# One Hymba layer on one core: the output projection as two groups of 1024 columns, with block sums made in DRAM

## The chip, the cores and the metric

The kernel runs on one core of one Trainium2 chip. The metric is the device time of one execution in microseconds (us); the kernel before has a median of 661.75 us in three runs (661.68 to 662.39). Everything is float32 in DRAM.

## The reference, cut to what matters

One layer for 512 tokens and a model width of 2048: an RMS norm, one input projection to 4608 columns, eight attention heads (two key and value heads) beside a gated linear recurrence (LRU) of width 1024, each group normed and gated, and one output projection with the residual.

```python
h = rms_norm(x, norm_w)                                  # 512 x 2048
q, k, v, g_attn, xr, g_lru = split(h @ w_in)             # w_in 2048 x 4608
attn_out = attention_group(q, k, v, q_norm_w, k_norm_w)  # 512 x 1024
lru_out = lru_group(xr, conv_w, conv_b, ...)             # 512 x 1024
mixed = concat([rms_norm(attn_out, attn_norm_w) * silu(g_attn),
                rms_norm(lru_out, lru_norm_w) * silu(g_lru)])
return x + mixed @ w_out                                 # w_out 2048 x 2048
```

## The kernel before, in words

Every product is made in three matmuls of split operands: a float32 operand is cast to a rounded form `hi` (on ACT) and the rest `lo` = operand - `hi` is taken (on DVE), and `hi hi`, `hi lo` and `lo hi` are added in PSUM. For weights this is `wsplit` (L209 the cast `wh`, L210 the difference `wl`), with buffers that TensorE releases.

The program has these stages: the input projection with the transposes and the norm of x; the LRU half by half beside the projections of its gate input, keys and values, and queries; attention beside the projections of the gates (names `fill`, `gates`); then the group norm of attention; the last gate projection; and the output projection from 495.03 us on. TensorE has work all the time, since projections are woven into the rest. The order on each engine is made by the scheduler of the language at build time from the order of the program and from priorities (`tc.high_priority(AHEAD)` and `SOON` move work ahead); each engine then works its list strictly in order. SP issues the loads, POOL does a few small operations (L261 and L262: scale, add and power of -0.5, which is an inverse root).

The group norm (`group_rstd`, `rows`): eight matmuls with ones (L662) bring the sums of squares `asum` into PSUM; DVE copies them to `r_a` (L666); POOL makes the inverse root (L261, L262); DVE makes `part` (L272, L273) and from these two diagonal tiles `s` (L275); TensorE turns the tiles into rows (L281) and DVE copies them to `gbc` (L282), by which the attention tiles are scaled (`normed`, L673). Between `group_rstd` and `rows` TensorE has three steps of six matmuls of the projection `fill`.

The output projection multiplies the mixed values (K = 2048 as eight row pairs of 2 x 128) with `w_out` by Winograd's form of Strassen's scheme: a pair's 2 x 2 blocks are combined into seven products P1, Q6, Q5, Q7, P2, Q3, Q4 in place of eight. The blocks of the mixed side are combined by `build` (function `seven`: sums in a tile `t`, L691 to L698; casts `mh`, L706; differences `ml`, L707). The four LRU pairs `hp` are built first, between steps of the projection that follows `rows`; the attention pairs `ap_` follow after their gate. The blocks of `w_out` are combined on DVE. The first 1024 columns are made as two groups of 512 by `outputs` (six pairs by Winograd with halves of 256 columns: 252 matmuls 128x256 for each group, and two pairs plainly: 48 matmuls 128x512). The other 1024 columns are one group of two halves of 512 by `outputs_wide`: 336 matmuls 128x512 in two passes over the pairs (P1, Q6, Q5, then Q3, P2, Q7, Q4). A gate is a sigmoid on ACT and two products on DVE (`gate`, L648, L652, L653); `evac` (L380) takes a projection out of PSUM.

Within attention, POOL scales each tile of weights (L588) before TensorE transposes it (L595).

## Time and profile before

| what | us |
|---|---|
| median of three runs | 661.75 |
| lowest, highest | 661.68, 662.39 |
| the profiled execution | 660.99 |
| its span | 659.2 |
| TensorE busy | 652.4 |
| DVE, ACT, POOL busy | 500.8, 337.4, 58.9 |
| output stage | 495.03 to 654.01 |

The profiled execution's own time is 1.8 us longer than its span, the stretch from its first to its last recorded event. Busy times are sums over an engine's instructions. A row of the time order has start, duration, engine, line, operation, what is written and read, and in brackets the idle time before it with the instruction that ended it. Grouped rows end with busy time, mean ns and the idle time before.

### The profile page before, as it was taken

To read this page: it belongs to the slowest core of one execution; us is meant where nothing else is said; L and a number is where in the kernel's file an instruction comes from. 1 tells how busy PE (TensorE), PEld (TensorE's weight loads), DVE (VectorE), ACT (ScalarE), POOL (GpSimd) and SP (SyncE) were. 2 spreads that over 40 slices of the span, in tenths; PEclk is the share of its full clock that TensorE was granted. 3 is DMA by queue.
4 is the path that set the end of the run, shared out by engine and by line. 5 is a ranking of instruction groups with operands and counts; after the bars stand their busy time and mean duration, and the time that the engine had idled before them with its cause. 6 is when DMAs were issued, how large, how long until landed. Compare 5 with 4: busy or idle time off the path is not lost.

```text
span 659.2 us, 8994 instructions
## 1 busy us (share of the span) xinstructions
PE 652.4 (99%) x3323; PEld 553.2 (84%) x3323; DVE 500.8 (76%) x822; ACT 337.4 (51%) x582; POOL 58.9 (9%) x79
## 2 busy tenths in 40 slices
PE   8999999999999999999999999999999999999996
PEld 6888888888888888888888888888889999888875
DVE  5889788978688854656955677439989998777995
ACT  3534898589766416444743455335437433233431
POOL 0000000000023303011222212110000000000000
PEclk9999999999999999999999999999999999999999
DMA  8852252323234312322112211232336356375643
GB/s 290 287 142 84 69 164 66 94 64 96 72 121 129 108 53 64 96 65 64 38 60 64 65 45 53 64 96 76 103 110 211 127 178 224 110 230 201 243 140 127
DMA packets 43963, 77.32 MB, mean 117 GB/s; under 512 B 2968, under 2 KB 13328, under 8 KB 43920
## 3 DMA queue, kind: packets, MB, share of 16 engines
q1 hardware_dynamic: 43600, 76.22, 37.5%
q10 hardware_dynamic: 320, 0.53, 0.3%
q8 instruction: 26, 0.43, 0.3%
q14 instruction: 17, 0.14, 0.1%
HBM read 72.54 MB, written 4.19 MB: 116 GB/s over the span
## 4 chain that ended last, share of the span: by engine, by line
PE 98%; DMA 1%; DVE 0%; ACTq 0%; DVEq 0%; issue 0%
PE pj L148 20%; PE pj L150 20%; PE pj L149 20%; PE pj L851 7%; PE pj L752 5%; PE mm L851 5%; PE mm L752 4%; PE mm L148 3%; PE mm L150 3%; PE mm L149 3%; PE mm L765 3%; PE mm L595 2%; PE mm L235 1%; PE pj L301 1%; PE mm L538 1%; DMA wr<-in_w_in_dram 1%
## 5 line engine op out<-in xcount | busy, mean ns | idle before, releaser
L148 PE MATMUL pj<-x,wh 128*128 128x512 f32 x376 | 149.1, 396 | 0.0
L150 PE MATMUL pj<-x,wl 128*128 128x512 f32 x376 | 147.0, 391 | 0.0
L149 PE MATMUL pj<-x,wh 128*128 128x512 f32 x376 | 146.5, 390 | 0.0
L210 DVE TENSOR_TENSOR wl<-wr,wh 128x512 fp32r<-128x512 f32 x144 | 100.8, 722 | 30.0 <-ACT wh L209 29.9
L209 ACT CAST wh<-wr 128x512 fp32r<-128x512 f32 x143 | 85.8, 618 | 73.4 <-PE pj L150 25.7
L150 PEld LDWEIGHTS pj<-x,wl 128*128 128x128 f32 x376 | 70.6, 188 | 15.3
L149 PEld LDWEIGHTS pj<-x,wh 128*128 128x128 f32 x376 | 70.7, 188 | 13.6 <-DVE x L238 0.2
L148 PEld LDWEIGHTS pj<-x,wh 128*128 128x128 f32 x376 | 70.6, 188 | 13.3
L148 PE MATMUL pj<-wh,x 128*128 128x512 f32 x192 | 74.9, 390 | 0.0
L150 PE MATMUL pj<-wh,x 128*128 128x512 f32 x192 | 74.7, 389 | 0.0
L149 PE MATMUL pj<-wl,x 128*128 128x512 f32 x192 | 74.7, 389 | 0.0
L841 ACT CAST wh<-wr 128x1024 fp32r<-128x1024 f32 (+1 forms) x24 | 28.7, 1198 | 52.0 <-PE mm L851 28.6
L597 ACT CAST b<-mm 128x512 fp32r<-128x512 f32 x32 | 18.8, 586 | 61.5 <-PE mm L595 61.5
L583 DVE TENSOR_REDUCE mx<-mm 128x1 f32<-128x512 f32 x32 | 22.0, 689 | 32.9 <-PE mm L150 32.3
L150 PEld LDWEIGHTS pj<-wh,x 128*128 128x128 f32 x192 | 36.0, 188 | 7.6
L148 PEld LDWEIGHTS pj<-wh,x 128*128 128x128 f32 x192 | 36.0, 188 | 7.5
L149 PEld LDWEIGHTS pj<-wl,x 128*128 128x128 f32 x192 | 36.0, 188 | 7.4
L588 POOL TENSOR_SCALAR k<-k,sm 128x512 f32<-128x512 f32 x32 | 24.2, 756 | 123.9 <-DVE sm L587 112.4
L842 DVE TENSOR_TENSOR wl<-wr,wh 128x1024 fp32r<-128x1024 f32 (+1 forms) x24 | 33.5, 1395 | 1.5 <-ACT wh L841 1.3
L598 DVE TENSOR_TENSOR b<-mm,b 128x512 fp32r<-128x512 f32 x32 | 22.1, 689 | 12.1 <-ACT b L597 12.1
L752 PE MATMUL pj<-wh,ml 128*128 128x256 f32 x96 | 27.2, 283 | 0.0
L752 PE MATMUL pj<-wl,mh 128*128 128x256 f32 x96 | 27.2, 283 | 0.0
(249 smaller groups left out, 1350.7 us busy)
## 6 DMA issues: line engine op xcount, KB each, us to landing
wr<-in_w_in_dram SPq DMA_DIRECT2D x71, 512.0 KB, 3.7
wr<-in_w_out_dram SPq DMA_DIRECT2D x40, 512.0 KB, 3.9
b<-in_x_dram SPq DMA_DIRECT2D x7, 512.0 KB, 8.9
out_dram<-xt SPq DMA_DIRECT2D x12, 256.0 KB, 3.2
xt<-in_x_dram SPq DMA_DIRECT2D x8, 256.0 KB, 5.0
wr<-in_w_out_dram SPq DMA_DIRECT2D x8, 256.0 KB, 4.3
t<-in_x_dram SPq DMA_DIRECT2D x4, 512.0 KB, 4.4
k<-in_lru_wa_dram SPq DMA_DIRECT2D x8, 128.0 KB, 3.6
```

Of the source, the lines that this page charges most:

```text
L148: nc.tensor.matmul(acc, lh, rh, start=start, stop=False)
L149: nc.tensor.matmul(acc, lh, rl, start=False, stop=False)
L150: nc.tensor.matmul(acc, ll, rh, start=False, stop=stop)
L209: copy(hi, raw[:, k, :])
L210: nc.vector.tensor_sub(lo, raw[:, k, :], f(hi))
L583: nc.vector.tensor_reduce(mx, sc, axis=AX.X, op=ALU.max, negate=True)
L588: nc.gpsimd.tensor_scalar(p, p, sm, 0.0, op0=ALU.mult, op1=ALU.add)
L598: nc.vector.tensor_sub(ptl[:, :, tt], p3, f(pth[:, :, tt]))
L752: nc.tensor.matmul(dst, lh[:, a, ts_], rh[:, b_, :], start=bank in fresh, stop=last and s == 1 and rh is bh and lh is al, skip_group_check ...
L841: nc.scalar.copy(hi, blocks)
L842: nc.vector.tensor_sub(lo, blocks, f(hi))
L851: nc.tensor.matmul(dst[s], lh[:, ts_], rh, start=i == 0 and j == 0, stop=i == 7 and j == 2)
```

## The change

All 2048 output columns go through one form: `outputs(0)` and `outputs(1)`, each 1024 columns in halves of 512, with all eight pairs by Winograd's form. The first pass holds P1, Q6, Q5, Q7 in all eight banks of PSUM (24 matmuls a pair), the second Q3, P2, Q4 (18 a pair): 2 x 8 x 42 = 672 matmuls of 512 columns, where there were 504 of 256 and 432 of 512.

Some sums of `w_out` blocks are made in DRAM. T3 (`t30`, `t31`, for both groups) and T1 (`t1`, group 0 alone) begin as copies from DRAM to DRAM on SP (24 of 256 KB), woven into the projections of the LRU stage. A transfer on POOL's queue that adds to its destination makes T3 (16, at the same place) and T1 (8, after the last queries' inverse roots and ahead of attention). T2, a sum that DVE makes in the first pass, is stored to DRAM on POOL's queue and read back in the second. The residual x and the outputs of group 0 go over POOL's queue too.

A gate takes Silu in place of the sigmoid, and one operation on DVE in place of two. The builds of the four LRU pairs stand ahead of `group_rstd` in the program, and the pools of attention are closed, and the pool `fin` opened, before it. Pairs 6 and 7 are built by `seven` as the others; `last_sums` is gone.

```diff
+    loads_done, powers = {}, []
     def wraw(w, r0, c0, nk=1, queue=nc.sync):
...
-            queue.dma_start(raw[:, ks, :], src[:, ks, :])
+            loads_done[queue] = queue.dma_start(raw[:, ks, :], src[:, ks, :]).ins
...
         nc.gpsimd.tensor_scalar(dst, src, 1.0 / n, EPS, op0=ALU.mult, op1=ALU.add)
-        nc.gpsimd.tensor_tensor(dst, dst, nhalf[:, :width], op=ALU.pow)
+        powers[:] = [nc.gpsimd.tensor_tensor(dst, dst, nhalf[:, :width], op=ALU.pow).ins]
...
-                    nc.scalar.activation(s, src, AF.Sigmoid)
+                    nc.scalar.activation(s, src, AF.Silu)
             s = ss[e] if sig is k2 else ss[0]
             yield 4
             dst = pairs[e // 2][:, e % 2, :]
-            nc.vector.scalar_tensor_tensor(g, g, v1(row + e), s, op0=ALU.mult, op1=ALU.mult)
-            nc.vector.tensor_mul(dst, dst, g)
+            nc.vector.scalar_tensor_tensor(dst, dst, v1(row + e), s, op0=ALU.mult, op1=ALU.mult)
...
+    split_of = [0]
+    def split(blocks):
+        i = split_of[0] % 4
+        split_of[0] += 1
+        hi, lo = (
+            pools["out" if i else "fin"].tile([P, 2, SEQ], F32R, tag=f"{t}{i}", bufs=1, name=nm(t))
             for t in ("wh", "wl")
...
+        hi, lo = (t[:, : blocks.shape[1]] for t in (hi, lo))
+        nc.scalar.copy(hi, blocks)
+        nc.vector.tensor_sub(lo, blocks, f(hi))
+        return hi, lo
...
+    dram = ctx.enter_context(tc.tile_pool(name="dram", bufs=1, space=bass.MemoryType.DRAM))
+    t1, t2, t30, t31 = (
+        dram.tile([NP, P, SEQ + 16], F32, name=t, tag=t)[:, :, :SEQ] for t in ("t1", "t2", "t30", "t31")
+    )
+    t3 = (t30, t31)
+    def block(m, k, c, n=1):
+        return w_out[(2 * m + k) * P : (2 * m + k + 1) * P, c * SEQ : (c + n) * SEQ]
+    def sums_of_blocks():
+        for m in range(NP):
+            with tc.issue_after(loads_done[nc.sync]):
+                for g in range(2):
+                    nc.sync.dma_start(t3[g][m], block(m, 0, 2 * g))
+                nc.sync.dma_start(t1[m], block(m, 0, 0))
+            for g in range(2):
+                nc.gpsimd.dma_start(t3[g][m], block(m, 1, 2 * g), accum_op=ALU.add)
+            yield
+    def other_sums():
+        with tc.issue_after(*powers):
+            for m in range(NP):
+                nc.gpsimd.dma_start(t1[m], block(m, 0, 1), accum_op=ALU.add)
+    def outputs(g, places, work):
...
+        p1, q6, q5, q7 = banks(*((mm, mm, pj, pj), (pj, mm, mm, pj))[g])
         for i in range(8):
+            m = mixed[i][0] // (2 * P)
+            with tc.high_priority(SOON):
+                x_, y_ = next(places)(), next(places)()
+                if g == 0:
+                    nc.sync.dma_start(x_[:, 0], t1[m])
+                    nc.sync.dma_start(x_[:, 1], block(m, 0, 1))
+                else:
+                    nc.sync.dma_start(x_.rearrange("p j e -> p (j e)"), block(m, 0, 2 * g, 2))
+                    nc.vector.tensor_add(x_[:, 0], x_[:, 0], x_[:, 1])
+                nc.sync.dma_start(y_[:, 0], block(m, 1, 2 * g))
+                nc.sync.dma_start(y_[:, 1], t3[g][m])
+                xb = split(x_)
+                nc.vector.tensor_add(y_[:, 0], y_[:, 0], x_[:, 0])
+                yb = split(y_)
+                nc.gpsimd.dma_start(t2[m], y_[:, 0])
+            next(work, None)
+            for k, dst, b, n in ((P1, p1, xb, 1), (Q6, q6, yb, 0), (Q5, q5, xb, 0), (Q7, q7, yb, 1)):
                 product(k, dst, i, b, n)
...
+            for s in range(2):
+                nc.vector.tensor_add(xs[0][:, s], q7[s], xs[0][:, 2 + s])
+                nc.vector.tensor_sub(xs[1][:, s], xs[1][:, s], q7[s])
+        def leave(t, j, queue, e0=0, e1=SEQ):
+            c0 = (2 * g + j) * SEQ
+            queue.dma_start(of[tokens[t], c0 + e0 : c0 + e1], xs[j][:, t, e0:e1])
...
+        q3, p2, q4 = banks(*((mm, mm, pj), (pj, mm, mm))[g])
...
+                x_ = ring.tile([P, 2, SEQ], F32, name=nm("wr"))
+                z_ = ring.tile([P, 1, SEQ], F32, name=nm("wr"))
+                nc.sync.dma_start(x_.rearrange("p j e -> p (j e)"), block(m, 1, 2 * g, 2))
+                nc.sync.dma_start(z_[:, 0], t2[m])
+                b = split(x_)
+                nc.vector.tensor_add(z_[:, 0], z_[:, 0], x_[:, 1])
+                z = split(z_)
+            return [
+                lambda: product(Q3, q3, i, b, 0),
+                lambda: product(P2, p2, i, b, 1),
+                lambda: product(Q4, q4, i, z, 0),
+            ]
+        for i in range(8 - 2 * g):
+            for step in second(i):
                 step()
             if 1 <= i < 5:
                 residual((i - 1) // 2, (i - 1) % 2)
+            if i == 1:
+                for t in range(2):
+                    leave(t, 0, nc.gpsimd)
+        if g:
+            for steps in zip(second(6), second(7)):
+                for step in steps:
+                    step()
         with tc.high_priority(SOON):
+            for t0, j, acc in ((2, 0, q3), (2, 1, p2), (0, 1, q4)):
+                for s in range(2):
+                    cut = 2 if g and acc is q4 and s else 1
+                    for e0 in range(0, SEQ, SEQ // cut):
+                        e1 = e0 + SEQ // cut
+                        to = xs[j][:, t0 + s, e0:e1]
+                        nc.vector.tensor_add(to, to, acc[s][:, e0:e1])
+                        leave(t0 + s, j, nc.sync if g else nc.gpsimd, e0, e1)
...
+    wsums = sums_of_blocks()
+    def with_sums(fill, n):
+        for k, _ in enumerate(fill):
+            if k % n == 0:
+                next(wsums, None)
+            yield
+    fill = with_sums(fill, 8)
...
-    weave(kv_proj(), lru_half(1, a2))
+    weave(with_sums(kv_proj(), 8), lru_half(1, a2))
...
     drain(fill)
+    other_sums()
...
     weave(fill, attention(rots))
+    closed("att", "qkv")
+    opened("fin", "right")
+    for shape, tag, bufs in (
+        [([P, 2, SEQ], t + "0", 1) for t in ("wh", "wl")]
+        + [([P, SEQ], "s", 2), ([P, SEQ], "ev", 4)]
+        + [([P, 7, H], f"{t}{i}", 1) for i in (3, 2, 1, 0) for t in ("mh", "ml")]
+        + [([P, 4, H], "t4", 2)]
+    ):
+        pools["fin"].tile(shape, F32, tag=tag, bufs=bufs, name=nm(tag))
+    mixed = [[(NH + 2 * q) * P, None] for q in range(4)] + [[2 * q * P, None] for q in range(4)]
+    def build(i, pair, parts):
+        mixed[i][1] = parts
+        seven(pair, *parts)
+    for q in range(4):
+        build(q, hp[q], kept("fin", q))
     for _ in range(6):
         next(fill)
     r = group_rstd(sums["a"], "r_a", NH * HD)
-    closed("att", "qkv")
-    opened("fin", "right")
     for _ in range(3):
         next(fill)
     rows(gbc, r, lambda: fin_s((P, NT, P), F32R))
...
-    for q in range(4):
-        for _ in range(2):
-            next(fill, None)
-        build(q, hp[q], lambda n: kept(pools["fin"]))
     drain(fill)
...
-    outputs(0, last_gates())
-    outputs(1, last_sums())
-    outputs_wide(2, *built)
+    def in_wr():
+        return wring.tile([P, 2, SEQ], F32, name=nm("wr"))
+    def in_av():
+        return aring.tile([P, 2, SEQ], F32, name=nm("wr"))
+    def in_kept(tag):
+        return lambda: pools["out"].tile([P, 2, SEQ], F32, tag=tag, bufs=1, name=nm("wr"))
+    turns = [in_wr] * 3 + [in_av]
+    outputs(
+        0, iter(turns + [in_kept(t + i) for i in "67" for t in ("mh", "ml")] + turns * 2), last_gates()
+    )
+    outputs(1, iter(([in_av] * 4 + [in_wr] * 3) * 3), iter(()))
```

The places in the engines' order that the prediction speaks of follow. Line numbers of the changed kernel are two or three higher here than those of the kernel before, up to the norm. First, DVE at the group norm, before: the copy `r_a` comes right behind the two splits `wl` of an earlier pair of matmuls, and the steps `t` of two builds stand among the chain to the tiles `s`.

```order
L210 TENSOR_TENSOR wl_4296<-wr_4293,wh_4295 128x512
L210 TENSOR_TENSOR wl_4300<-wr_4293,wh_4299 128x512
L666 COPY r_a<-mm_4249 128x4
L696 TENSOR_TENSOR t_887_4317<-hs_868 128x512
L272 CAST part_4281<-r_a 128x4
L696 TENSOR_TENSOR t_890_4339<-hs_1065 128x512
L273 TENSOR_TENSOR part_4282<-r_a,part_4281 128x4
L275 TENSOR_TENSOR s_4283<-ident,part_4281 128x512
L275 TENSOR_TENSOR s_4284<-ident,part_4282 128x512
```

The same place now, with the end of the four builds (`t_885`, `t_888`, `ml`) and the splits of the projection's next tile `wr_4440`, whose first matmuls TensorE has behind those with `s`:

```order
L696 TENSOR_TENSOR ml_4278<-t_885_4279,mh_4277 128x1024
L213 TENSOR_TENSOR wl_4443<-wr_4440,wh_4442 128x512
L213 TENSOR_TENSOR wl_4447<-wr_4440,wh_4446 128x512
L693 TENSOR_TENSOR t_888_4289<-hs_1704,t_888_4289 128x256
L668 COPY r_a<-mm_4353 128x4
L275 CAST part_4380<-r_a 128x4
L276 TENSOR_TENSOR part_4381<-r_a,part_4380 128x4
L278 TENSOR_TENSOR s_4382<-ident,part_4380 128x512
L696 TENSOR_TENSOR ml_4288<-t_888_4289,mh_4287 128x1024
L278 TENSOR_TENSOR s_4383<-ident,part_4381 128x512
```

The copy `r_a` moved behind all four builds and behind the splits `wl_4443` and `wl_4447`, and one difference `ml` came between the two tiles `s`. TensorE's order around the norm is the same in both: the matmuls with ones, three steps of six, the two with `s`.

Second, DVE at the start of the output stage, before: the last evacuations `ev` and gates, then the splits of the second pair (those of the first are done).

```order
L380 TENSOR_TENSOR ev_4685<-pj_4379,rbc 128x512
L653 TENSOR_TENSOR av_3578<-av_3578,ev_4681 128x512
L652 SCALAR_TENSOR_TENSOR ev_4683<-ev_4683,vec,s_4841 128x512
L380 TENSOR_TENSOR ev_4687<-pj_4380,rbc 128x512
L707 TENSOR_TENSOR wl_4764<-wr_4761,wh_4763 128x768
L707 TENSOR_TENSOR wl_4764<-t_973_4765,wh_4763 128x1024
```

The same place now; `wl_4709` is the last split of the last projection, `wr_4799` the sum of the second pair's blocks, and `wl_4770` the split that the first pair's second product (Q6) reads:

```order
L213 TENSOR_TENSOR wl_4709<-wr_4702,wh_4708 128x512
L790 TENSOR_TENSOR wr_4799<-wr_4799,wr_4798 128x512
L383 TENSOR_TENSOR ev_4736<-pj_4436,rbc 128x512
L383 TENSOR_TENSOR ev_4738<-pj_4437,rbc 128x512
L655 SCALAR_TENSOR_TENSOR av_3628<-av_3628,vec,s_4864 128x512
L383 TENSOR_TENSOR ev_4740<-pj_4438,rbc 128x512
L655 SCALAR_TENSOR_TENSOR av_3628<-av_3628,vec,s_4867 128x512
L383 TENSOR_TENSOR ev_4742<-pj_4439,rbc 128x512
L691 TENSOR_TENSOR t_1011_4914<-av_3628 128x512
L721 TENSOR_TENSOR wl_4770<-wr_4759,wh_4769 128x1024
```

A split of the first pair now stands behind the sum of the second pair, the last four evacuations, two gates and the first step of a build.

More of the change, by code (lines that the diff above doesn't have):

```diff
@@ L707, in seven @@
             nc.vector.tensor_sub(lo[:, to], part, f(hi[:, to]))
-    def four(src, hi, lo):
-        src = halves(src)
-        nc.scalar.copy(hi, src)
-        nc.vector.tensor_sub(lo, src, f(hi))
     def aside(tile_of, n):
@@ L717, in aside, with kept @@
         return t[:, 8 : 8 + n * H].rearrange("p (n e) -> p n e", e=H)
[L719 to L727 removed]
+    def kept(pool, i):
+        return [
+            pools[pool].tile([P, 7, H], F32R, tag=f"{t}{i}", bufs=1, name=nm(t))
+            for t in ("mh", "ml")
+        ]
@@ L909, in outputs_wide, with second @@
-        for i in range(6):
-            for step in plain(i):
+        q3, p2, q4 = banks(*((mm, mm, pj), (pj, mm, mm))[g])
+        def second(i):
+            m = mixed[i][0] // (2 * P)
+            ring = (wring, aring)[i % 2]
+            with tc.high_priority(SOON):
+                x_ = ring.tile([P, 2, SEQ], F32, name=nm("wr"))
[9 more added lines that the diff above has]
+                lambda: product(Q4, q4, i, z, 0),
+            ]
@@ L1032, in hybrid_kernel @@
     drain(fill)
+    other_sums()
     closed("rot", "rope", "wx")
[L1035 removed]
+    sums["a"] = const([P, SEQ], "asum")
     opened("att", "right")
@@ L1065, in hybrid_kernel @@
     rows(gbc, r, lambda: fin_s((P, NT, P), F32R))
-    mixed = [[(NH + 2 * q) * P, None] for q in range(4)] + [[2 * q * P, None] for q in range(4)]
-    sums_of, built = {}, []
-    def build(i, pair, where, n=7):
-        mixed[i][1] = hi, lo = where(n)
-        if n == 7:
-            seven(pair, ALU.subtract, hi, lo)
-        else:
-            four(pair, hi, lo)
-    for q in range(4):
-        for _ in range(2):
-            next(fill, None)
-        build(q, hp[q], lambda n: kept(pools["fin"]))
     drain(fill)
@@ L1092, in later @@
             yield next(todo)
-        build(4, ap_[0], lambda n: [hring.tile([P, n, H], F32R, name=nm(t)) for t in ("mh", "ml")])
+        build(4, ap_[0], [hring.tile([P, 7, H], F32R, name=nm(t)) for t in ("mh", "ml")])
         yield from todo
@@ L1107, in last_gates @@
         yield
-        build(5, ap_[1], lambda n: kept(pools["out"]))
+        build(5, ap_[1], kept("out", 5))
         yield
```

208 lines of the change are left out of this document (17 added, 191 removed).

## Prediction

> **What bounds the kernel now.** I read the page's busy table first, then its slices, then the chain of work that ended last.
>
> ```profile
> span 659.2 us, 8994 instructions
> PE 652.4 (99%) x3323; PEld 553.2 (84%) x3323; DVE 500.8 (76%) x822; ACT 337.4 (51%) x582; POOL 58.9 (9%) x79
> ...
> PEclk9999999999999999999999999999999999999999
> ...
> PE 98%; DMA 1%; DVE 0%; ACTq 0%; DVEq 0%; issue 0%
> ```
>
> TensorE is busy 652.4 of 659.2 us at full clock and carries 98% of the chain: it is packed from the first projection to the last product. So the time changes in only two ways: by the number and width of matmuls, and by any hole that opens in that row. No other engine's busy time matters by itself; DVE at 76% and ACT at 51% matter through what they deliver late.
>
> Width is priced by the windows of the output stage: a narrow group (its 252 Winograd matmuls, 256 columns wide), the wide group (336 matmuls, 512 wide), and the whole stage. Columns are length, PE busy (count), weight loads (count).
>
> ```profile
> 495.03:525.26 30.23, 30.23 (x252) 30.18 (x251) 1.00 0.54 169
> ...
> 577.31:653.80 76.49, 76.49 (x336) 62.73 (x335) 1.00 0.58 191
> ...
> 495.03:654.01 158.98, 158.98 (x937) 141.22 (x935) 136.54 (x169) 62.77 (x66) 0.00 (x0) 1.00 0.56 181
> ```
>
> One 256-wide matmul takes 30.23/252 = 0.120 us, one 512-wide 76.49/336 = 0.228 us: two narrow ones cost 0.240, one wide does the same columns for 0.228.
>
> **Part 1: all products 512 wide.** The two narrow groups have 504 matmuls of 256 and 96 of 512; the wide group 336 of 512. After: 672 of 512. The new stage is 672 x 0.2277 = 153.0 us against 158.98: **-6.0 us**. TensorE is the bound, so all of it counts.
>
> **Part 2: the builds of the four LRU pairs ahead of the group norm.** The rows around the norm, in time order (start, duration, engine, operation, wait):
>
> ```profile
> 441.55 0.16 DVE L666 COPY r_a<-mm 128x4 f32<-128x4 f32 x1 [0.97 <-PE mm L662]
> ...
> 441.80 0.56 POOL L261 TENSOR_SCALAR r_a<-r_a 128x4 f32<-128x4 f32 x1 [9.40 <-DVE r_a L666]
> ...
> 442.45 1.02 POOL L262 TENSOR_TENSOR r_a<-r_a,nhalf 128x4 f32<-128x4 f32 x1
> ...
> 443.50 0.17 DVE L272 CAST part<-r_a 128x4 fp32r<-128x4 f32 x1 [1.20 <-POOL r_a L262]
> ...
> 443.78 0.39 PE L149 MATMUL pj<-x,wh 128*128 128x512 f32 x1
> ...
> 444.18 0.15 DVE L273 TENSOR_TENSOR part<-r_a,part 128x4 f32<-128x4 f32 x1
> 444.26 1.28 DVE L275 TENSOR_TENSOR s<-ident,part 128x512 fp32r<-128x512 f32 x2
> ...
> 444.89 1.30 ACT L209 CAST wh<-wr 128x512 fp32r<-128x512 f32 x2 [2.10 <-PE pj L149]
> ...
> 445.37 0.39 PE L150 MATMUL pj<-x,wl 128*128 128x512 f32 x1
> 445.59 0.62 PE L281 MATMUL mm<-s,ones_r 128*128 128x512 f32 x2
> ...
> 446.67 0.68 DVE L210 TENSOR_TENSOR wl<-wr,wh 128x512 fp32r<-128x512 f32 x1
> ```
>
> and two groups of DVE from 438 to 462 (busy, mean ns of one | idle before), parts of the builds:
>
> ```profile
> L707 DVE TENSOR_TENSOR ml<-t,mh 128x1024 fp32r<-128x1024 f32 x3 | 3.6, 1212 | 0.0
> ...
> L697 DVE TENSOR_TENSOR t<-hs,t 128x256 f32<-128x256 f32 x3 | 1.2, 413 | 0.0
> ```
>
> (Seven starts from 443.78 to 445.37 make a step of 0.227; with it the new output stage is 152.5 us and part 1 gives -6.4, the far end.) The sum of squares leaves PSUM at 441.55 (copy `r_a`); POOL makes the root (441.80 to 443.47); DVE makes two tiles `s`, ready at 445.54; TensorE's two `s` matmuls start at 445.59 and 445.82. The spare is 0.05 us on the first and 0.28 at most.
>
> In the new DVE order all four builds, and the two splits `wl` for the pair of matmuls that TensorE runs after the `s` matmuls, stand ahead of that copy. Those splits cannot run early: their casts on ACT start at 444.89 when TensorE releases the buffers, and end at 446.19. TensorE's order is the same before and after, so that release does not move. The copy therefore waits for 446.19, the split (0.68), and one step of the last build (0.41): 447.3; with the builds' own casts queued on ACT I take 447.45, against 441.55. Then the chain as measured: copy to cast 1.95 us (443.50 - 441.55) gives 449.4; cast, difference, first `s` (0.17 + 0.15 + 0.64) gives 450.4; then a 1.21-us `ml` of the last build stands between the two tiles, and the second `s` (0.64) ends near 452.2. TensorE, due at 445.82, goes on at 452.2: **+6.35 us**, in two holes of about 4.8 and 1.5. Bounds: 5.9 if the copy goes at 447.3 and the 1.21 starts at once; 7.5 if ACT's casts are a further step late. Nothing gives this back before the output stage, since afterwards DVE and TensorE stand as far apart as they did. POOL has nothing else there; the PSUM copies behind (`gbc`) move with it.
>
> **Part 3: the first pair of the output stage.** Rows of DVE around its start at 495.03:
>
> ```profile
> 485.23 1.23 DVE L707 TENSOR_TENSOR wl<-t,wh 128x1024 fp32r<-128x1024 f32 x1 [1.11 <-ACT wh L706]
> 486.37 1.29 DVE L210 TENSOR_TENSOR wl<-wr,wh 128x512 fp32r<-128x512 f32 x2
> ...
> 493.87 0.69 DVE L380 TENSOR_TENSOR ev<-pj,rbc 128x512 f32<-128x512 f32 x1
> ...
> 494.48 0.68 DVE L653 TENSOR_TENSOR av<-av,ev 128x512 f32<-128x512 f32 x1
> ...
> 495.08 0.74 DVE L652 SCALAR_TENSOR_TENSOR ev<-ev,vec,s 128x512 f32<-128x512 f32 x1
> ...
> 495.75 0.68 DVE L380 TENSOR_TENSOR ev<-pj,rbc 128x512 f32<-128x512 f32 x1
> ```
>
> and the page's rows of the loads (KB each, us from issue to landing):
>
> ```profile
> wr<-in_w_in_dram SPq DMA_DIRECT2D x71, 512.0 KB, 3.7
> ...
> wr<-in_w_out_dram SPq DMA_DIRECT2D x8, 256.0 KB, 4.3
> ```
>
> Call the start S. Before, the first pair's splits ended at 486.46. After, P1's six matmuls and one of Q6 use what is there; the eighth, at S + 7 x 0.228 = S + 1.6, needs `wl_4770`. DVE's queue ahead of it: the sum `wr_4799` of the next pair, four `ev`, two gate operations, one build step. That is six at about 0.6 from start to start, two at 0.67, then the split of 1024 at 1.21: 6.2 us. The sum's block is loaded into a slot that the last weight splits free (before: 487.66, S - 7.4); two or three issues at 0.4 and a landing of 3.7 to 4.3 put it at S - 2.8 to S - 1.5. With S - 2.2, `wl_4770` ends at S + 4.0, **+2.4 us**. If the load is not late, the last `ev` (S + 0.3) binds: S + 2.7, +1.1; at S - 1.5 it is +3.1. I keep 1.1 to 3.1, and 0 if the stall of part 2 lets DVE run ahead here. The gate's Silu form takes 16 products off DVE; only the two in this queue are on the path, and they are left out above already.
>
> **Part 4: the transfers.**
>
> ```profile
> 36.94 5.09 SPq L198 DMA_DIRECT2D wr<-in_w_in_dram  x2
> ...
> 50.68 1.31 ACT L209 CAST wh<-wr 128x512 fp32r<-128x512 f32 x2 [2.33 <-PE pj L149]
> ...
> 262.11 1.32 POOL L262 TENSOR_TENSOR rr<-rr,nhalf 128x4 f32<-128x4 f32 x1
> ...
> 278.38 0.70 POOL L588 TENSOR_SCALAR k<-k,sm 128x512 f32<-128x512 f32 x1 [14.95 <-DVE sm L587]
> ...
> 282.14 0.60 PE L595 MATMUL mm<-ident,k 128*128 128x128 f32 x4
> ```
>
> On SP, 24 copies from DRAM to DRAM stand among the weight loads of the LRU phase, up to three ahead of one load. A load issued at 36.94 is read at 50.68; after a landing of 3.7 that leaves 10.0 us of cover, against three issues and one landing wait (1.3 + 3.7): 0. POOL's 16 accumulating transfers there stand in front of small root chains with micro-seconds of spare, taken as 0 to 3. Eight more stand between POOL's root ending at 263.43 and the first scaled tile at 278.38, which TensorE reads at 282.14: the idle is 14.95 and the spare behind it 282.14 - 279.08 = 3.06, so 18.0/8 = 2.25 us each are free. No accumulating transfer is in the trace. If POOL only issues them (SP's issues take about 0.43), they cost 0; if each is waited for at 4.3, 34.4 us against 18.0, +16.4. I take 0, since the issues of SP do not wait for landings, and keep 16 as the far end.
>
> The Trainium skill, "DMA: Bandwidth & Descriptors", section on the anatomy of one DMA, fits a transfer issued from POOL as about 2.0 us plus bytes over 436 GB/s; by that, an estimate, 256 KB take 2.6 us, and eight in sequence 20.9, which would make the sum 2.9 us longer. No row here shows it.
>
> The stored sum T2 is written in the first pass and read back in the second; for the last pair that is from 7 x 24 x 0.228 = 38 us to 44 + 7 x 18 x 0.228 = 73 us of the group: 0. Loading and summing in the output stage: DVE does less per pair than now (T3 and T1 arrive summed), so I take 0 for the three changes of pass, each 0 to 1.5. The last stores go through SP as before, so the 5 us behind the last matmul stay.
>
> **Sum.** -6.0 + 6.35 + 2.4 + 0 = +2.75 us. Profiled 660.99 becomes 663.7; the median of the runs, 661.75, stands 0.76 above that execution, so 664.5.
>
> **Rivals.**
>
> - A, other side: the copy `r_a` is not late, TensorE stays packed. For it: TensorE's order is unchanged and the chain of four small steps is short. Against it: the two splits ahead of the copy wait for a release at 444.89. Time: 661.75 - 6.0 = 655.7. It decides from the point where the copy goes less than 6.0 us late, with part 3 at zero.
> - B: part 2 holds and part 3 is absorbed: 661.75 - 6.0 + 6.35 = 662.1, no measurable change.
> - C: the clock drops in the new hole.
>
> ```profile
> 1.12 3.10 PE L951 MATMUL mm<-ones 128*128 128x256 bf16 x14 [1.12 <-POOL ones L156]
> ...
> 655.00:659.20 4.20, 0.00 (x0) 0.00 (x0) 0.00 (x0) 0.00 (x0) 0.00 (x0) 1.00 0.43 126
> ```
>
> The first 14 matmuls, 256 wide, run at 3.10/14 = 0.221 us, nearly twice the 0.120 of later ones: a slow stretch that costs 1.4 us, or up to twice that around a 4.8-us hole. Against it: behind the last matmul (the stage's end at 654.01) the granted clock is still 1.00 up to 659.20, 5 us. Time: 664.5 + 1.4 to 2.8, about 666.5.
>
> The Trainium skill, "TensorE: Matmul & The Clock Gate", section on the oscillation, allows no idle gap above some 3.4 us before the clock halves. By that rule this hole would cost C's price; the 5 us at full clock do not bear it out, though the window it names runs freely and may have missed them.
>
> - D: transfers are late, at POOL's eight (+3 to +16) or at the changes of pass (three times up to 1.5): 667 to 680.
>
> **Chances.** Forecast (662.7 to 665.8 by the bounds of part 3 and 0.4 on part 2) 0.48; B 0.14; C 0.17; D 0.11; A 0.10. About 0.2%, 1.3 us, is what a measurement of this kernel can tell from no change: 660.4 to 663.1. Faster is A, 0.10; same is B and the low edge of the forecast, 0.17; slower the rest, 0.73. The range 661.2 to 668.5 leaves out A and most of D.
>
> **What would show it.** After: 211 matmuls of 256 columns instead of 715; the copy `r_a` about 5.9 us later against the same projection; TensorE idle 4 to 5 us and then 1 to 2 us ahead of the two `s` matmuls, with DVE as releaser; a hole of 1 to 3 us before the eighth product of the output stage; the stage's matmuls alone at 153 us. Wrong if TensorE shows no hole at the norm (then near 656), or if POOL's tile at 278.38 comes later.

## The result: 4.1% slower

The median after is 689.65 us (687.52 to 690.94, four runs) against 662.07 (661.68 to 662.39) before: ratio 1.0414, 95% interval 1.0384 to 1.0443. The profiled execution took 688.86 us, of which the span is 687.1. The forecast of 664.5 had the right sign and a tenth of the size: the profiled span grew by 27.9 us where +2.75 was expected.

The page after, its busy table, the first row of its slices, and the accumulating transfers:

```profile
PE 660.7 (96%) x3059; PEld 543.8 (79%) x3059; DVE 482.7 (70%) x788; ACT 340.2 (50%) x590; POOL 97.1 (14%) x137
...
PE   9998999999999999999999999979989989889997
...
t<-in_w_out_dram POOLq DMA_DIRECT2D x24, 256.0 KB, 6.2
```

TensorE has 264 matmuls fewer, as the widths say, and yet is busy 8.3 us longer. DVE, the next busiest engine, is *less* busy than before (482.7 against 500.8 us), ACT is at 50% and POOL at 14%, so no engine's load explains it. TensorE's row has dents: one early, one at the group norm, and several in the output stage. The windows cut the span at them (length, busy us and count of PE, PEld, DVE, ACT, POOL, then granted clock, DMA share, GB/s); first after, then before:

```profile
0.00:57.70 57.70, 56.51 (x278) 45.88 (x279) 38.26 (x126) 22.16 (x37) 5.24 (x15) 1.00 0.79 247
57.70:64.30 6.60, 3.75 (x11) 2.71 (x10) 6.18 (x16) 1.84 (x3) 0.75 (x1) 0.74 0.78 159
64.30:450.80 386.50, 386.50 (x1883) 323.78 (x1881) 278.02 (x444) 231.08 (x449) 69.74 (x86) 1.00 0.38 104
450.80:460.20 9.40, 4.38 (x11) 2.99 (x11) 6.43 (x13) 2.94 (x3) 1.23 (x2) 0.64 0.17 56
460.20:507.58 47.38, 47.38 (x210) 39.20 (x209) 25.64 (x38) 14.13 (x22) 1.23 (x2) 1.00 0.43 131
507.58:682.24 174.66, 162.01 (x673) 129.22 (x671) 127.19 (x155) 68.10 (x77) 18.96 (x32) 0.96 0.66 215
```

```profile
0.00:445.59 445.59, 443.84 (x2169) 371.07 (x2170) 316.75 (x581) 252.93 (x487) 58.90 (x79) 1.00 0.32 97
445.59:495.03 49.44, 49.44 (x219) 40.92 (x218) 46.55 (x72) 21.72 (x31) 0.00 (x0) 1.00 0.32 96
```

A window counts every matmul that reaches into it. Up to the norm 450.80 against 445.59: +5.2, of which the hole at 57.7 has 4.5 (nine steps from start to start, from 57.71 to 64.28, take 6.57 us, and at 0.227 they take 2.0). The other 0.7 is there by 46 us (the transpose L184 starts at 46.41, before at 45.74), and its cause stays open. From the norm to the output stage 56.78 against 49.44: +7.3. The stage 174.66 against the 158.98 shown above: +15.7. The tail is 0.3 shorter. That is all of the 27.9. In the first two dents the granted clock falls too (0.74, 0.64): behind each hole some matmuls start 0.427 us apart instead of 0.227. In the output stage it is 0.96 over the whole.

**At the norm** the rows are those that were forecast (in time order; start, duration, operation, wait):

```profile
450.14 1.31 ACT L212 CAST wh<-wr 128x512 fp32r<-128x512 f32 x2 [0.52 <-PE pj L149]
...
450.58 0.39 PE L150 MATMUL pj<-x,wl 128*128 128x512 f32 x1
...
450.80 1.38 DVE L213 TENSOR_TENSOR wl<-wr,wh 128x512 fp32r<-128x512 f32 x2
...
452.43 0.15 DVE L668 COPY r_a<-mm 128x4 f32<-128x4 f32 x1
...
454.90 1.22 DVE L696 TENSOR_TENSOR ml<-t,mh 128x1024 fp32r<-128x1024 f32 x1
455.04 0.79 PE L284 MATMUL mm<-s,ones_r 128*128 128x512 f32 x1 [4.08 <-DVE s L278]
...
456.78 0.80 PE L284 MATMUL mm<-s,ones_r 128*128 128x512 f32 x1 [0.94 <-DVE s L278]
```

The copy `r_a` waits for the splits, those for the casts, those for a release by TensorE; the root is late by the same amount and one `ml` parts the two tiles. The matmul starts after the last projection matmul (450.58 to 455.04, then to 456.78) are 4.46 and 1.74 us apart instead of 0.227: holes of 4.24 and 1.51.

**At 57.7**, in the LRU phase, where I had put the transfers at nothing:

```profile
43.86 1.92 POOL L744 DMA_DIRECT2D t<-in_w_out_dram  x2 [42.22 <-DMA t<-in_w_out_dram]
44.94 3.08 SPq L394 DMA_DIRECT2D k<-in_lru_wx_dram  x4
...
46.13 1.04 POOL L265 TENSOR_TENSOR rstd<-rstd,nhalf 128x4 f32<-128x4 f32 x1
...
53.23 0.62 ACT L408 CAST k<-k 128x512 fp32r<-128x512 f32 x1 [2.53 <-DMA k<-in_lru_wx_dram]
53.88 0.69 DVE L409 TENSOR_TENSOR k<-k,k 128x512 fp32r<-128x512 f32 x1 [2.48 <-ACT k L408]
...
60.11 1.29 DVE L383 TENSOR_TENSOR ev<-pj,rbc 128x512 f32<-128x512 f32 x2
60.95 0.77 PE L148 MATMUL pj<-x,wh 128*128 128x512 f32 x1 [2.85 <-DVE ev L383]
```

The same root and evacuation before, and the landing of these four loads (KB each, median us from issue to landing), before and then after:

```profile
41.77 1.04 POOL L262 TENSOR_TENSOR rstd<-rstd,nhalf 128x4 f32<-128x4 f32 x1
...
54.60 1.29 DVE L380 TENSOR_TENSOR ev<-pj,rbc 128x512 f32<-128x512 f32 x2
...
k<-in_lru_wx_dram SPq DMA_DIRECT2D x4, 128.0 KB, 3.5
...
k<-in_lru_wx_dram SPq DMA_DIRECT2D x4, 128.0 KB, 8.0
```

Two things come late together. POOL's first accumulating transfers wait for SP's copies into the same DRAM rows, and POOL's root stands behind them: 4.4 us later. SP's copies stand ahead of the LRU weight loads `k`, so the cast of those weights waits for them, and DVE's split of the cast, which stands ahead of the evacuation `ev`, waits for the cast. The evacuation is 5.5 us late, and TensorE needs the bank it frees. The loads are issued only 0.8 us later than before (44.94 against 44.12); the larger part of their delay is the landing, 8.0 us against 3.5, with copies and accumulating transfers on their way at the same time. Whether they are slow by their place in the queue or by a shared rate, these rows do not tell apart.

**In the output stage**, the rows on DVE and TensorE at one change of pass:

```profile
557.87 0.69 DVE L836 TENSOR_TENSOR wr<-wr,wr 128x512 f32<-128x512 f32 x1 [2.46 <-DMA wr<-t]
558.48 1.28 DVE L801 TENSOR_TENSOR cb<-cb,mm 128x512 f32<-128x512 f32 x2
...
562.07 0.39 PE L771 MATMUL mm<-wh,mh 128*128 128x512 f32 x1
...
563.27 1.82 DVE L721 TENSOR_TENSOR wl<-wr,wh 128x1024 fp32r<-128x1024 f32 x2
564.54 0.50 PE L771 MATMUL mm<-wl,mh 128*128 128x512 f32 x1 [2.08 <-DVE wl L721]
```

and what DVE waits for in the stage (total us, times, longest):

```profile
DVE wr L836 <- DMA wr<-t: 18.8, 10, 3.0
DVE wr L790 <- DMA wr<-in_w_out_dram: 8.7, 7, 2.6
DVE wr L786 <- DMA wr<-in_w_out_dram: 7.4, 5, 3.3
DVE wr L790 <- DMA wr<-t: 6.9, 2, 6.3
```

DVE stands 41.8 us at the sums of loaded blocks (the three kinds of sum: L786, L790, L836). In DVE's order such a sum, of a *later* pair, comes ahead of splits `wl` that TensorE needs soon; when its block has not landed, the work whose data lie ready waits behind it: here the eight evacuations of the pass (558.48 to 563.27) and behind them the split for which TensorE stands.

### The profile page after: what moved, and what is told of

Read it like the earlier page. It is cut to its first block, busy times and chain, and to the rows that moved or that the text cites. A ratio compares the mean times of both kernels' runs of the same rounds, so it can differ in the third digit from the quotient of the medians.

```text
span 687.1 us, 8648 instructions
## 1 busy us (share of the span) xinstructions
PE 660.7 (96%) x3059; PEld 543.8 (79%) x3059; DVE 482.7 (70%) x788; ACT 340.2 (50%) x590; POOL 97.1 (14%) x137
## 2 busy tenths in 40 slices
DMA packets 54140, 100.38 MB, mean 146 GB/s; under 512 B 4568, under 2 KB 14928, under 8 KB 54096
## 5 line engine op out<-in xcount | busy, mean ns | idle before, releaser
L720 ACT CAST wh<-wr 128x1024 fp32r<-128x1024 f32 x64 | 60.0, 944 | 99.3 <-PE mm L771 61.3
L148 PEld LDWEIGHTS pj<-x,wh 128*128 128x128 f32 x376 | 71.4, 190 | 16.8 <-issue 3.2
L149 PEld LDWEIGHTS pj<-x,wh 128*128 128x128 f32 x376 | 71.4, 190 | 14.0 <-DVE x L241 0.3
L721 DVE TENSOR_TENSOR wl<-wr,wh 128x1024 fp32r<-128x1024 f32 x64 | 67.2, 1085 | 9.3 <-ACT wh L720 9.1
L771 PE MATMUL mm<-wl,mh 128*128 128x512 f32 x128 | 51.9, 406 | 5.9 <-DVE wl L721 5.8
L771 PE MATMUL mm<-wh,mh 128*128 128x512 f32 x128 | 51.2, 400 | 1.9 <-ACT wh L720 1.9
L771 PE MATMUL mm<-wh,ml 128*128 128x512 f32 x128 | 51.2, 400 | 0.0
L586 DVE TENSOR_REDUCE mx<-mm 128x1 f32<-128x512 f32 x32 | 22.1, 690 | 33.2 <-PE mm L150 32.4
L771 PE MATMUL pj<-wl,mh 128*128 128x512 f32 x96 | 39.0, 407 | 4.8 <-DVE wl L721 4.8
```

Source lines behind the costliest of these rows:

```text
L148: nc.tensor.matmul(acc, lh, rh, start=start, stop=False)
L149: nc.tensor.matmul(acc, lh, rl, start=False, stop=False)
L586: nc.vector.tensor_reduce(mx, sc, axis=AX.X, op=ALU.max, negate=True)
L720: nc.scalar.copy(hi, blocks)
L721: nc.vector.tensor_sub(lo, blocks, f(hi))
L771: nc.tensor.matmul(dst[s], lh[:, ts_], rh, start=i == 0 and j == 0, stop=i == 7 and j == 2)
```

## The experiments

Three theories for the 27.9 us. T1: each dent has its own cause, order at the norm (+7.3), queues at 57.7 (+4.5), the sums in the output stage (the rest). T2: the extra 23 MB of traffic (100.38 MB against 77.32) makes all transfers late, and the order matters little. T3: the clock is the loss and the holes are only where it shows. All ratios below are to the kernel before, on the same chip.

**e1: the builds behind the norm again.**

```diff
-    for q in range(4):
-        build(q, hp[q], kept("fin", q))
     for _ in range(6):
         next(fill)
 ...
     rows(gbc, r, lambda: fin_s((P, NT, P), F32R))
+    for q in range(4):
+        for _ in range(2):
+            next(fill, None)
+        build(q, hp[q], kept("fin", q))
```

> The changed kernel with the four LRU builds put back behind the group norm, between the steps of the projection. Theory (each stall is a cost of its own, and a hole of several us also halves TensorE's clock for a while): the holes of 4.24 and 1.51 us at the norm and the half clock behind them go, so about 7.3 us less than the 689.65 of the changed kernel: 682.3, with TensorE's row packed from 440 to 500 us. Rival (DVE is simply short of time after attention, and the delay comes back at the next place): 687 to 690, with a larger hole at the start of the output stage.

679.66 us, ratio 1.0261 (1.0243 to 1.0279): 10.0 us less than after. The window over the norm is packed at full clock:

```profile
446.00:501.00 55.00, 55.00 (x246) 45.56 (x246) 38.17 (x61) 19.69 (x29) 2.55 (x4) 1.00 0.45 135
```

The 7.3 us at the norm are gone; what more it gained came from somewhat smaller holes in the output stage (171.2 us long in its profiled execution, 174.7 in that of after).

**e2: the same move in the kernel before, alone.** Attention's pools are closed ahead of the builds, as in the change. The sum of squares is kept in the row `gbc`, by which the LRU pairs are scaled, so that this scaling works with other numbers; the instructions are the same. This holds for e7 too.

```diff
-    sums["a"] = pools["qkv"].tile([P, SEQ], F32, tag="asum", name="asum")
+    sums["a"] = gbc
 ...
+    for q in range(4):
+        build(q, hp[q], lambda n: kept(pools["fin"]))
     for _ in range(6):
         next(fill)
     r = group_rstd(sums["a"], "r_a", NH * HD)
 ...
-    for q in range(4):
-        for _ in range(2):
-            next(fill, None)
-        build(q, hp[q], lambda n: kept(pools["fin"]))
```

> The kernel before with one part of the change alone: the four builds ahead of the group norm, and attention's pools closed ahead of it; the sum of squares lives in the tile gbc until gbc is written. Output stage as before. Theory: two holes at the norm, 5.5 to 6.4 us together, and 1.4 to 2 us of half clock behind them, nothing given back: 662.07 + 7.0 to 8.4 = 669 to 670.5. Rival (the holes are absorbed later, or the clock does not drop): 662 to 668.5.

670.31 us, ratio 1.0121 (1.0106 to 1.0136), +8.1 us. TensorE's waits at the `s` matmuls are those of after, 4.07 and 0.94, and the window has the same half clock:

```profile
450.91 0.80 PE L281 MATMUL mm<-s,ones_r 128*128 128x512 f32 x1 [4.07 <-DVE s L275]
...
446.60:457.10 10.50, 5.49 (x14) 3.80 (x13) 7.51 (x14) 3.32 (x5) 1.22 (x2) 0.67 0.18 50
```

So part 2 needs nothing else of the change: no transfer, no new width.

**e7: e2 with the hole filled by 30 matmuls that compute nothing used.** This parts the hole from the clock.

```diff
         pb = mm()
+        for _ in range(idle):
+            nc.tensor.matmul(pb[:, : 2 * P], wv[:, :P], wv, start=True, stop=True)
 ...
-    rows(gbc, r, lambda: fin_s((P, NT, P), F32R))
+    rows(gbc, r, lambda: fin_s((P, NT, P), F32R), 30)
```

> The kernel before with the builds ahead of the norm (as run alone earlier: 670.31), and 30 idle-work matmuls of 256 columns, about 3.6 us, put on TensorE ahead of the two s matmuls, where it stood idle for some 4.5 us. They write the bank that the s matmuls start afresh. Theory (the idle time itself costs 6.1, and a hole of over 3 us costs another 1.8 of half clock): the half clock goes, 670.3 - 1.8 = 668.5. Rival (the half clock is no matter of the idle hole): 670.3 or a little more.

```profile
446.20 3.45 PE L280 MATMUL mm<-ones 128*128 128x256 bf16 x30
450.42 0.49 PE L283 MATMUL mm<-s,ones_r 128*128 128x512 f32 x1 [0.77 <-DVE s L275]
...
445.60:456.10 10.50, 8.48 (x52) 6.63 (x51) 8.41 (x14) 4.14 (x5) 1.21 (x2) 1.00 0.18 50
```

The `s` tiles come as late as in e2, the clock stays at 1.00, and from the last projection matmul ahead of `s` to the twentieth matmul behind it 10.85 us pass instead of 12.87 (before: 5.01). The half clock was thus 2.0 of the 7.9 us there. The times, 668.60 (1.0107, 1.0090 to 1.0123) against 670.31 (1.0121), lie that way, but their intervals overlap: the trace shows it, the time alone does not. T3 takes a quarter of the loss at the norm, not the loss; over all five dents with a drop of the clock it is 9.3 of the 27.9 us (last section).

**e3: POOL's accumulating transfers behind the root; e4: SP's copies behind the LRU weight loads.**

```diff
-            for g in range(2):
-                nc.gpsimd.dma_start(t3[g][m], block(m, 1, 2 * g), accum_op=ALU.add)
+            with tc.issue_after(*powers):
+                for g in range(2):
+                    nc.gpsimd.dma_start(t3[g][m], block(m, 1, 2 * g), accum_op=ALU.add)
```

> The changed kernel with the first accumulating transfers of POOL ordered behind the inverse root of the input's norm (before it they stood ahead and waited 42.22 us of idle POOL for SP's copies, and the root ended 4.4 us later than in the kernel before). Theory: the hole of 3.0 us at 57.7 us has two causes in a row, POOL's root (3.0 us later at the first small DVE steps) and the LRU weights loaded late by SP (2.5 us of idle DVE), against 2.5 us of spare; with POOL's share gone the hole shrinks under 0.5 us and the half clock goes: 3.5 to 4.5 us less, 685 to 686. Rival (the loads behind SP's copies alone set it): hole of 2.5 us or more stays, 688.5 to 690.

e3: 687.90 us, ratio 1.0383 (1.0359 to 1.0408), which overlaps the interval of after and is above the 685 to 686 that I expected. In the trace the hole falls to two small ones (0.73 us of idle here, 0.93 five us later) with no half clock:

```profile
58.54 0.47 PE L148 MATMUL pj<-x,wh 128*128 128x512 f32 x1 [0.73 <-DVE ev L383]
```

So POOL's queue is a part of the cause and not all of it. e4 takes the other part; with the copies later, POOL's transfers come behind the root without an edit of their own.

```diff
-            with tc.issue_after(loads_done[nc.sync]):
+            with tc.issue_after(loads_done[nc.sync]), tc.issue_after(loads_done[2]), tc.issue_after(loads_done[3]):
```

(`loads_done[2]` and `[3]` are set at the last load `lru_wx` of these two LRU blocks.)

> The changed kernel with the copies from DRAM to DRAM ordered on SP behind the loads of the first LRU weights (the transfers of POOL then come behind the inverse root by themselves). Theory: both causes of the hole at 57.7 us go, 4.5 us less: 685.2, and TensorE's row is packed up to 440 us. Rival (the transfers' traffic as such slows the loads, wherever they stand): a hole stays or moves, 687 to 690.

e4: 682.97 us, ratio 1.0317 (1.0291 to 1.0343), 6.7 below after. The stretch is packed, and the last projection matmul ahead of `s` starts at 445.75 (before 445.37, after 450.58):

```profile
20.00:445.70 425.70, 425.70 (x2075) 356.52 (x2074) 311.17 (x549) 246.79 (x476) 75.00 (x92) 1.00 0.44 119
```

All the copies and accumulating transfers still run, in these 425.70 us, and the loads `k` land after 3.7 us instead of 8.0: against T2 as the cause of the whole, though at this one place the transfers did make a load late. Some 4.8 of the 6.7 lie ahead of the norm; the rest stays open, and this kernel's runs spread over 4 us.

**e5: e1 and e4 together.**

> The changed kernel with both earlier edits together: builds behind the group norm, and the copies of SP behind the loads of the first LRU weights. Theory (the stalls are independent and add): 689.65 - 10.0 - 6.7 = 673, with TensorE packed from 20 us to the output stage, and what is left over the kernel before is the output stage alone. Rival (one earlier stall hid part of another): 676 or more.

674.81 us, ratio 1.0207 (1.0190 to 1.0224). The two gains, 10.0 and 6.7, add up nearly (14.8). What is left, 13.4 us above before in spite of the width, is the output stage (it starts at 495.65, before at 495.03).

**e6: e5 with each sum of blocks issued behind the split directly ahead; e8: behind the split before that one.** Nothing else moves: the same loads, rings and traffic. The edit of e8 (e6 keeps only the newest split, so that the list has one entry):

```diff
-        nc.vector.tensor_sub(lo, blocks, f(hi))
+        last_split[:] = [*last_split[-1:], nc.vector.tensor_sub(lo, blocks, f(hi)).ins]
+    def add_late(dst, a, b):
+        if last_split:
+            with tc.issue_after(last_split[0]):
+                nc.vector.tensor_add(dst, a, b)
+        else:
+            nc.vector.tensor_add(dst, a, b)
 ...
-                nc.vector.tensor_add(y_[:, 0], y_[:, 0], x_[:, 0])
+                add_late(y_[:, 0], y_[:, 0], x_[:, 0])
```

(the sums into `x_` and `z_` likewise)

> The kernel of the run beside it (both stalls out), with one more edit in the output stage: each block sum on DVE is ordered directly behind the split before it, where the scheduler had put sums of later pairs ahead of splits that TensorE needs at once. Theory (DVE waits in order at early sums whose blocks have not landed; the changed kernel's DVE stood 42 us at such sums in the stage): most holes of the output stage go, 6 to 12 us less than the run beside it, about 661 to 667. Rival (the loads are late in any order, because of ring slots and traffic): within 2 us of the run beside it, 671 to 675.

e6: 669.67 us, ratio 1.0132 (1.0115 to 1.0149), above what was expected. The sums no longer wait for transfers, but now each split waits for its cast, since the cast can only start when the sum right ahead of the split is done:

```profile
DVE wl L722 <- ACT wh L721: 30.6, 31, 2.3
```

> As the kernel with the sums in turn (669.67), but each block sum is ordered behind the split before the last, not the last: one sum ahead, so that the cast on ACT of one block can run beside DVE's split of another. Theory (with the sums strictly in turn DVE waits some 31 us for casts, a chain of sum, cast and split for each block): the small holes of 0.5 to 1.2 us in the steady passes go, 4 to 6 us less, 664 to 666; the large hole between the two groups (3.5 and 2.6 of half clock) stays. Rival (DMA again: sums that are one ahead wait for their blocks): 669 to 673.

e8: **655.52 us, ratio 0.9907 (0.9890 to 0.9923)**, faster than both kernels and 8.5 to 10.5 us below what I expected of it; the hole between the two groups, which I expected to stay, is gone too. One sum in advance lets ACT's cast run beside another split and seldom makes the sum wait for its block: DVE's waits are 15.4 us for casts (30.6 in e6) and 4.0 for blocks (41.8 in after). Its transfers and the stage's window:

```profile
DMA packets 54140, 100.38 MB, mean 154 GB/s; under 512 B 4568, under 2 KB 14928, under 8 KB 54096
...
495.46:649.00 153.54, 152.62 (x673) 125.86 (x671) 125.59 (x153) 66.94 (x75) 19.57 (x33) 1.00 0.74 245
```

The stage takes 153.54 us with the same 100.38 MB in the whole, at a higher rate (245 GB/s against 215). With all the traffic TensorE is packed, so T2 is out. TensorE stands 0.92 us in all in that window, at the first pair.

**e10: the order of the sums alone, in the changed kernel.** The edit is that of e8, without e1 and e4.

> The changed kernel with the one edit of the output stage alone (each block sum behind the split before the last), the norm and the LRU stage as changed. Theory (three separate stalls): with both other stalls out this edit took 674.81 to 655.52, so here too 19.3 us less than 689.65: 670.4, with the holes at the norm and at 57.7 us unmoved. Rival (the stalls before the stage shift the loads and DVE, so that the edit finds less to gain): 674 or more.

667.55 us, ratio 1.0087 (1.0069 to 1.0105), 22.1 below after, somewhat more than the 19.3 expected. The norm keeps its dent (9.40 us for the same matmuls, as in after), the stage is as short as in e8:

```profile
507.30:661.10 153.80, 152.88 (x673) 125.79 (x671) 125.90 (x153) 66.97 (x75) 19.50 (x33) 1.00 0.74 244
```

The same 673 matmuls: 20.9 us less, of which 11.7 is idle time (12.65 to 0.92) and 9.1 a longer busy time of the same matmuls (162.01 to 152.88), for the larger part at the half clock. What separates e10 from e8, 12.0 us, is about the norm's 7.3 and the 4.5 at 57.7: T1's parts add up.

**e9: e8 with four further edits at the changes of pass** (the evacuation of `q7` after pair 1, pair 1's `z_` sum behind that of `q5`, the residual added one pair later, a higher priority for the first pair's loads).

```diff
+        def q7_out():
             for s in range(2):
 ...
+            if i == 1:
+                q7_out()
+            if 1 < i < 6:
+                to_add()
```

> As the kernel with sums one ahead, and the changes of pass eased: the evacuation of Q7 after the second pair of the second pass, that pair's sum behind the evacuation of Q5, the residual added one pair after its load was issued, the first pair of a group with the priority of the projections. Theory (what is left in the output stage are bursts of 8 evacuations, 4.8 us of DVE, ahead of splits, and waits for the residual): 655 to 661, at or below the kernel before. Rival (loads and casts bind there, not DVE's order): within 2 us of the kernel with sums one ahead.

659.78 us, ratio 0.9975 (0.9957 to 0.9993): inside the range expected, but 4.3 worse than e8, on which it was to improve. In the profiled execution, the slowest of ten (663.10), DVE waits at a residual whose load is late, and the split behind it is late for TensorE:

```profile
563.54 1.22 DVE L832 TENSOR_TENSOR cb<-cb,t 128x1024 f32<-128x1024 f32 x1 [5.13 <-DMA t<-in_x_dram]
...
565.96 0.50 PE L779 MATMUL mm<-wl,mh 128*128 128x512 f32 x1 [4.22 <-DVE wl L722]
```

Which of the four edits made that load late stays open; the mechanism is again a waiting instruction in front of a ready one.

## Why the prediction was right in sign and wrong in size

- **Part 1, the width, -6.0: right.** The stage without the misplaced sums takes 153.54 us (e8) and 153.80 (e10) where 153.0 was worked out and 158.98 stood before. With the two other stalls out, the whole kernel takes 655.52; rival A, with TensorE packed, had 655.7.
- **Part 2, builds ahead of the norm, +6.35: right in its mechanism, a little off in its size.** Holes of 4.24 and 1.51 where about 4.8 and 1.5 were forecast (5.75 against the bounds 5.9 to 7.5; the copy went 0.98 us behind the end of the splits' casts, where I had 1.26), then 1.6 to 2.0 us of half clock (ten steps, 450.58 to 460.17, lose 7.3 us, less the holes; e7). +7.3 in after; alone in the kernel before +8.1 (e2). The chain of waits named in advance is the one in the trace, row by row.
- **Rival C, the clock, 0.17: it happened**, and in five dents, not one. Its price of 1.4 to 2.8 a hole was right (1.5 to 2.8 in after, 2.0 in e7). The argument against it, full clock for 5 us behind the last matmul, was worth nothing: the row showed the time behind the work, not matmuls that resume. The Trainium skill, "TensorE: Matmul & The Clock Gate", section on the oscillation, was the better guide here in kind: the clock fell after the 4.24-us hole. Its limit of some 3.4 us does not hold as a safe one, as the last section shows.
- **Part 3, the first pair, +2.4: right in its mechanism, at the top of its bounds, without the clock.** DVE waits 6.31 us at the second pair's sum, which it starts 1.7 us ahead of the stage where I had 2.2; the four evacuations, two gate operations and the build step follow, and then the split. TensorE stands for 1.87 us and a little later for 0.67:

```profile
505.91 0.69 DVE L790 TENSOR_TENSOR wr<-wr,wr 128x512 f32<-128x512 f32 x1 [6.31 <-DMA wr<-t]
...
509.35 0.63 ACT L651 ACTIVATE s<-ev 128x512 f32<-128x512 f32 x1 [0.89 <-DVE ev L383]
...
510.97 0.67 PE L771 MATMUL mm<-wh,mh 128*128 128x512 f32 x1 [1.87 <-ACT wh L720]
512.30 0.80 PE L771 MATMUL mm<-wl,mh 128*128 128x512 f32 x1 [0.67 <-DVE wl L721]
```

  The eighth matmul starts 4.7 us into the stage (512.30 less 507.58), where S + 4.0 was forecast: 3.1 late against the forecast 2.4, the upper bound. One reading was wrong: "one of Q6" does not use what is there. The seventh matmul already stands, for its cast `wh`, which ACT starts at 509.89, behind the gates' activations (L651), and these wait for the same late evacuations `ev`. Behind the holes the clock is halved (0.50 from 511.13 to 517.96), which adds another 2.8, so 5.9 in all against 1.1 to 3.1.
- **Part 4, "0" for the transfers: here the prediction failed**, in two of its sentences. "against three issues and one landing wait (1.3 + 3.7): 0" looked up the cover of TensorE's weight loads on SP and of no other load in that queue. The root chains behind POOL's transfers it did name ("micro-seconds of spare, taken as 0 to 3"), but it put them into the sum as 0 without a row for the spare. The LRU weight loads behind the copies, which landed after 8.0 us, and POOL's root behind accumulating transfers that must wait for those copies, were the ones without cover: 4.5 us at 57.7 (e4 takes 4.8 off the time up to the norm). And "I take 0 for the three changes of pass, each 0 to 1.5", because DVE does less per pair than before, was about 16 us with the clock (the 20.9 us between the stages of after and e10, less the 4.8 by which the first pair's dent shrank): it argued from an engine's load where its order decides. The order of the changed kernel shows sums of later pairs ahead of splits that TensorE reads next. I had used just that reading for the first pair, and left it out for those behind. e10 shows that this order alone cost 22.1 us, part 3 included.
- **POOL's eight transfers ahead of attention, 0 with a far end of +16.4: right, but not with the margin that 0 suggests.** The row from 64.30 to 450.80 is packed with all eight in it. Yet they hold POOL for 15.7 us (268.60 to 284.32) of the 18.0 that were free, 2.0 us each, where "If POOL only issues them" had SP's 0.43. The estimate from the Trainium skill, "DMA: Bandwidth & Descriptors", section on the anatomy of one DMA, was 2.6 us for 256 KB issued from POOL; measured, an accumulating one lands after 6.2 (median). (By that fit eight in sequence are 20.8 us, not the 20.9 that I wrote.) Eight waited for in turn would be 50 us; so POOL does not wait for each to land, except where what it adds to is still being written, which is what happened at 57.7.
- **Rival D, transfers late, 0.11, 667 to 680:** the right place with a price too small, since it was worked out as three events of up to 1.5. Behind the first pair's, the stage has seven dents of 0.4 to 2.6 us of idle time, two of them with a drop of the clock.

## What to carry to other kernels

An in-order engine at 70% can hold up a packed TensorE: for each instruction that waits for a transfer, ask which ready instructions stand behind it, at every repetition and not only the first. The place of a sum among the splits can be both too early (41.8 us of waits for blocks) and too late (30.6 us of waits for casts); one split of lead was the best of the three orders tried, and was worth 22.1 us of 689.65. When transfers are added to a queue, the cover to look up is that of every load and every small chain that comes behind them, and a dependence between two queues makes all the work behind it on the second one wait (POOL's root, 4.4 us).

## What the runs showed of the hardware

- **The clock falls after holes shorter than expected, and not after every one of a size.** TensorE stands idle for 2.08 us at 562.07 and for 2.01 at 591.30; the first hole has a drop of the clock behind it, the second has none. Stretches of 3.41 us around the two (length, PE busy and count, granted clock, DMA share, GB/s):

```profile
562.33:565.75 3.42, 1.34 (x6) 1.00 0.06 11
565.75:569.16 3.41, 3.41 (x9) 0.50 0.53 154
...
589.64:593.05 3.41, 2.05 (x10) 1.00 0.91 326
593.05:596.47 3.42, 2.77 (x12) 1.00 0.68 210
```

  The Trainium skill, "TensorE: Matmul & The Clock Gate", section on the oscillation, names some 3.4 us for the idle gap; the drop behind 2.08 us is below that, and here the measurement decides. That the window runs freely, as the same page has it in its section on what is actually happening, fits the difference. The five slow stretches of after last 3.41 us or twice that, and they begin on one grid, at 60.57, 453.11, 511.13, 565.75 and 606.71: the last four are 17, 16 and 12 times 3.413 us apart. Divided by this grid, the hole of 2.08 us lies in one stretch and leaves 1.34 us busy in it; the hole of 2.01 is parted between two (1.36 and 0.65 idle). In all the traces here every full-speed stretch of the grid with 1.87 us idle or more is followed by a slow one, none with 1.52 or less is, and between these both occur. By starts against 0.227 us a step, the five drops of after cost 1.5 to 2.8 us each on top of their holes, 9.3 in all.
- **Work that computes nothing holds the clock** (e7): 30 matmuls in the hole, and the row reads 1.00 instead of 0.67.
- **A transfer that accumulates in DRAM does not hold its queue until it lands, but it can hold it by what it depends on.** POOL's idle time of 42.22 us ahead of the first two (43.86) ended with a copy's landing; the two were then issued in 1.92 us, and POOL went on to its root at 45.85, well within the 6.2 us that one takes to land. Of the eight ahead of attention, the first three are issued in 2.62 us and the other five 1.4 to 2.6 us from start to start; what paces those five, the profile does not name for most of them.
